# Queries on partitions for all heads of a decoder block, stores on GpSimd's queue, gating weights kept

## The chip, the cores and the metric

The kernel runs on one core of a Trainium2 chip. The metric is the device time of one execution in microseconds; the median of three runs is given. One further execution was profiled, and all rows of the trace come from it. TensorE multiplies matrices, VectorE, ScalarE and GpSimd work element by element, and SyncE only issues transfers; each engine takes its instructions in order and waits where a result is missing.

## What is computed

One decoder layer on 2048 tokens of width 1024 in float32. Half of the mixer is attention with eight heads of 64, each a mixture of three dilated windows; the other half is a spatial gating unit. A SwiGLU network follows. Each half is wrapped in RMS norms.

```python
DILATED_PATTERNS = ((128, 1), (512, 4), (2048, 16))
def dilated_mixture_attention(q, k, v):
    ...
    for window, dilation in DILATED_PATTERNS:
        o, lse = dilated_window_attention(q, k, v, window, dilation)
        ...
    wts = jax.nn.softmax(jnp.stack(lses, axis=0), axis=0)
    o = jnp.sum(wts[..., None] * jnp.stack(outs, axis=0), axis=0)
...
h = rms_norm(x, pre_mix_norm[l])
proj = h @ w_in[l]
q, k, v_a, u, v_s = jnp.split(proj, ...)
...
attn = dilated_mixture_attention(q, k, v_a)
sgu = spatial_gating(u, v_s, ...)
mixed = jnp.concatenate([rms_norm(attn, attn_out_norm[l]), rms_norm(sgu, sgu_out_norm[l])], axis=-1)
x = x + rms_norm(mixed @ w_out[l], post_mix_norm[l])
h = rms_norm(x, pre_ffn_norm[l])
f = (jax.nn.silu(h @ w_gate[l]) * (h @ w_up[l])) @ w_down[l]
x = x + rms_norm(f, post_ffn_norm[l])
```

## The kernel before

The tokens are cut into four blocks of 512 (m = 0 to 3), and the attention into two halves of 1024 queries (x = 0 for blocks 0 and 1, x = 1 for blocks 2 and 3). To keep float32 accuracy with a faster product, each operand is split into a high part and the rest (`w_hi`, `w_lo`; `ah`, `al`; `ph`, `pl`), and a dense product is three products: high by high, rest by high, high by rest. A weight block is loaded by `wtile` (L167) as `w_raw`, copied to `w_hi` by ScalarE and subtracted to `w_lo` by VectorE; where the same block is needed again, `w_lo` is stored in DRAM (`wc`) and comes back by `wcached` (L189). `group` (L204) runs the dense products of one projection (all of them have line L212) into four banks `d` and hands each bank to an `evac`.

The program has these parts. Up to 165 us of the span: in_proj of k, q and v for blocks 0 and 1. From 165 to 747 ("stage 2"): the gating unit of all blocks (`ip_su` L476, `ip_gate` L512), the reload of block 0's normalised input from `hD` (`ip_again` L397), in_proj of blocks 2 and 3, all merged with `tq_heads(0)`. From 747 to 1545 ("stage 3"): out_proj of blocks 0 and 1, the first three parts of the feed-forward network and the up projection of its second half, merged with `heads(1)`. Then out_proj of blocks 2 and 3, the last down projection, and from 1850 on a part that the change leaves alone (`st_up`, `st_down`).

The two halves of the attention are written in two ways. `heads(1)` (L1631) has keys on partitions: `scores` (L665) multiplies 256 queries at a time against a block of 128 keys (L728, L729), adds the mask (L736) and keeps a running maximum `macc`; `mix` (L753) subtracts the maximum, takes the exponential, splits into `ph` and `pl`, and multiplies with the values (L809, L811), again 256 queries at a time. `tq_heads(0)` (L1013) has queries on partitions: `tq_scores` (L934) multiplies 128 queries against up to 512 keys (L963, L964), VectorE reduces to a minimum per query and ScalarE takes the exponential with it; `tq_turn` (L974) transposes the weights by TensorE in blocks of 128 (L1003, L1006) and splits them, and `pv` (L1056, L1057) multiplies with the values, mostly 128 columns at a time. At the end of each pair of heads `tq_merge` (L1114) passes small tables through DRAM (`rr`, `tqC`, `ww`, then the weights `ws` and `wn`), which takes four transfers one behind the other.

A scheduler sets the order in which instructions stand on each engine. `merge` interleaves two generators by the numbers of steps given (L1652: 133 x 1.2 steps for the first heads, L1662), `high_priority` raises some instructions, and a tile's `bufs` says how many buffers it has: a load into a tile stands in the order where a buffer of it comes free. Every transfer, load or store, is issued by `dma` (L146, issue at L151) on SyncE. An evacuation of k, q or v writes into four `io` buffers and stores eight pieces per group of four banks (L447 to L464). `out_rows` (L1178) evacuates the rows of out_proj and of the down projection to `y`, adds the residual row `xr`, which it loads `ahead` rows in advance, and stores the result; in stage 3 there is one `xr` buffer and `ahead` is 1.

```python
            v.scalar_tensor_tensor(yj, yj, r, xs[i], ALU.mult, ALU.add)
            self.dma(dst[j * P:(j + 1) * P, 512 * n:512 * n + 512], yj)
            ...
            fetch(i + ahead)
```

Of the kernel before, what the change touches and what calls it, by code (L numbers as in the profile page):

```python
# [10 lines left out]
F32 = mybir.dt.float32  # L11
# [67 lines left out]
HP_Q = 200  # L79
# [5 lines left out]
XR = 1  # L85
T_LAG = 2
T_END = 3
HP_T = 0
# [4 lines left out]
R1 = 1.2  # L93
# [19 lines left out]
class Body:  # L113
# [38 lines left out]

    def rstd(self, ss, n, inv_n, eps, name, parts=P):
# [13 lines left out]
    def wtile(self, src, perm=False, shape=None, save=None, pool=None, bufs=None):  # L167
# [17 lines left out]
        if save is not None:  # L185
            self.dma(save, lo)
# [179 lines left out]
    def ip_load2(self, c, pool):  # L366

        self.seen[c] = True
        w_in = self.t["w_in"][0].rearrange("(k p) c -> k p c", p=P)
        kept = {}  # L370

        def load(k):
            kept[k] = self.wtile(w_in[k, :, c * 512:(c + 1) * 512], perm=c < 2, pool=pool, bufs=W_KEPT)
            return kept[k]

        def again(k):
            self.dma(self.wc[c][k], kept[k][1])
            return kept.pop(k)

        return load, again  # L380
# [9 lines left out]
    def ip_keep(self, m):  # L390

        for k in range(KT):
            for i in range(2):
                self.dma(self.hD[k, i], self.h[m][i][k])
                yield

    def ip_again(self, m):  # L397

        h = self.ip_tiles(m, self.ip)
        for k in range(KT):  # L400
            for i in range(2):
                self.dma(h[i][k], self.hD[k, i])
            yield
# [27 lines left out]
    def ip_kq(self, m, sec, load, tabs):  # L431
# [3 lines left out]
        def evac(b, ps):  # L435
# [14 lines left out]
            self.dma(scr[0][b * P:(b + 1) * P, :], oh)  # L450
            self.dma(scr[1][b * P:(b + 1) * P, :], ol)
# [3 lines left out]
    def ip_v(self, m, load):  # L455
        nc, pool, v = self.nc, self.ip, self.nc.vector

        def evac(b, ps):
            pv = ps.rearrange("p (h e d) -> p h e d", h=4, e=2)
            for e in range(2):  # L460
# [3 lines left out]
                self.dma(self.vD[m][e::2, b * P:(b + 1) * P, :].rearrange("h p d -> p h d"),  # L464
# [47 lines left out]
    def ip_gate(self, m):  # L512
# [4 lines left out]
        ws = pool.tile([P, 2, 8, P], F32R, name="ws", tag="big", bufs=4)  # L517
        self.dma(ws, self.wsD)
# [25 lines left out]
        for ft in range(4):  # L544
# [5 lines left out]
            self.dma(self.sT[m][ft], o)  # L550
# [11 lines left out]
    def attn_pools(self, pool):  # L562
        self.ap, self.lt = pool, "mt"
        self.cst = pool.tile([P, C_TRIL], F32, name="cst")
        self.dma(self.cst, self.t["consts"][:, 0:C_TRIL])

    def stacks(self, x, h):

        nc, pool = self.nc, self.ap
        nkm = 2 * (x + 1)  # L570

        def rows(scr):
            return scr.rearrange("(a h d) t -> h a d t", a=8, h=8)[h]

        qs = pool.tile([P, 4, 2, P], F32R, name="qs", tag="qs", bufs=1)
        ql = pool.tile([P, 4, 2, P], F32R, name="ql", tag="ql", bufs=1)
        ks = [pool.tile([P, TB], F32R, name="ks", tag="ks", bufs=4) for _ in range(nkm)]
        for mm in range(2):
            q = self.qT[2 * x + mm]
            for dst, src in ((qs[0:64], q[0]), (qs[64:128], q[0]), (ql[0:64], q[1]), (ql[64:128], q[1])):  # L580
                self.dma(dst[:, :, mm, :], rows(src))
        for m in range(nkm):
            for s in range(2):
                self.dma(ks[m][64 * s:64 * s + 64, :], rows(self.kT[m][s]))
        nf = 7 * x
        k1 = pool.tile([P, 8 + x, P], F32R, name="k1", tag="k1", bufs=1, padded_shape=[P, 9, P])
        for m in range(nf // 4, nkm):
            lo = max(nf, 4 * m)
            n = 4 * m + 4 - lo
            nc.gpsimd.tensor_copy(k1[:, lo - nf:lo - nf + n, :].rearrange("p j (r i) -> p j r i", r=4),  # L590
                                  ks[m].rearrange("p (r j i) -> p j r i", r=4, j=4)[:, 4 - n:4])
        return ks, k1, nf, qs, ql

    def values(self, x, h):

        pool = self.ap
        nkm = 2 * (x + 1)
        v4 = [pool.tile([P, 4, P], F32R, name="v4", tag="v4", bufs=4) for _ in range(nkm)]
        n0 = 0 if x == 0 else 7
        v1t = pool.tile([P, 8 * (x + 1) - n0, P], F32R, name="v1", tag="v1", bufs=1, padded_shape=[P, 9, P])  # L600
        v1 = {n: v1t[:, n - n0, :] for n in range(n0, 8 * (x + 1))}
        for m in range(nkm):
            self.dma(v4[m].rearrange("p r d -> p (r d)"), self.vD[m][h].rearrange("(i r) d -> i (r d)", r=4))
            lo = max(n0, 4 * m)
            cnt = 4 * m + 4 - lo
            if cnt > 0:
                src = self.vD[m][h].rearrange("(j i r) d -> r i j d", r=4, i=32)
                for r in range(4):
                    self.dma(v1t[32 * r:32 * r + 32, lo - n0:lo - n0 + cnt, :], src[r, :, 4 - cnt:4])
        return v4, v1  # L610

    def lanes(self, acc, op, name):
# [4 lines left out]
        tr = self.ap.tile([P, 1024], F32, name=name + "_t", tag=self.lt, bufs=1)  # L617
# [7 lines left out]
    def to_row(self, src, dst, name):  # L625
# [3 lines left out]
        self.dma(dst.rearrange("(b a) -> b a", a=32), t)  # L629

    @staticmethod
    def qview(u, a):

        if u[1][0] == "s":
            o = u[1][1] * 256 + u[1][2] * 128
            return a[:, o:o + u[2]]
        return a.rearrange("p (r c) -> p r c", r=4)[:, :, 32 * u[1][1]:32 * u[1][2]]

    @staticmethod
    def uview(u, a, off):  # L640
        s = a[:, off:off + u[2]]
        return s if u[1][0] == "s" else s.rearrange("p (r c) -> p r c", r=4)

    @staticmethod
    def twins(us):

        return len(us) == 2 and us[0][2] == us[1][2] == 256

    def fold(self, us, s, acc, op, seen):

        if us[0][1][0] == "s" and us[0][1][1] not in seen:
            seen.add(us[0][1][1])
            o = us[0][1][1] * 256
            if self.twins(us):
                self.nc.vector.tensor_tensor(acc[:, o:o + 256], s[:, 0:256], s[:, 256:512], op)
            else:
                self.nc.scalar.copy(acc[:, o:o + 128], s[:, 128:256])
                self.nc.vector.tensor_tensor(acc[:, o + 128:o + 256], s[:, 256:384], s[:, 0:128], op)
            return
        off = 0  # L660
        for u in us:
            self.nc.vector.tensor_tensor(self.qview(u, acc), self.qview(u, acc), self.uview(u, s, off), op)
            off += u[2]

    def scores(self, x, h, st):  # L665

        nc, v, pool = self.nc, self.nc.vector, self.ap
        ks, k1, nf, qs, ql = self.stacks(x, h)
        yield
        qf, qlf = (t.rearrange("p r m i -> p (r m i)") for t in (qs, ql))  # L670
        q3, ql3 = (t.rearrange("p r m i -> p r (m i)") for t in (qs, ql))
        n0 = 8 * x
        tiles = []

        def keys4(r, m):
            return ks[m][:, r * P:(r + 1) * P]

        def keys1(n):
            return k1[:, n - nf, :]

        for r in range(4):
            for pr in range(x + 1):
                us = []
                for m in (2 * pr, 2 * pr + 1) if pr < x else (2 * pr + 1, 2 * pr):
                    last = m == 2 * x + 1
# [1025 lines left out]
```

## Time and profile before

| | |
|---|---|
| median of three runs | 2573.8 us (2573.55 to 2574.82) |
| profiled execution | 2575.44 us |
| its span | 2573.7 us |
| TensorE busy | 2328.9 us, 90% |
| VectorE busy | 1639.1 us, 64% |
| ScalarE busy | 1185.9 us, 46% |
| GpSimd busy | 364.4 us, 14% |
| mean granted clock of TensorE | 0.958 |
| transfers, mean | 186 GB/s, all of the kernel's on one queue (q1) |

A share over the span is an average over stages with different limits, so it is read together with windows by stage. The tables of waits give, for an engine, which instruction it stood before and what ended the wait last. In a timeline an engine's instructions stand in the order of their starts; since products are pipelined, a product's own time is longer than its distance to the next start.

### The profile page before, as it was taken

The page shows a single profiled execution, that of the slowest core. Times are in us where ns is not written, and L with a number is a line of the kernel's source. Part 1 is how long each engine was busy: PE and PEld are TensorE (multiplying, and loading weights), DVE is VectorE, ACT ScalarE, POOL GpSimd, SP SyncE. Part 2 cuts the span into 40 slices and gives each one's busy share as a digit, 9 for nine tenths or more (in the row PEclk, how much of TensorE's full clock was granted, in tenths as well). Part 3 has the DMA queues.
Part 4 walks back from the last instruction along what each step waited for, and adds up shares of the span by engine and source line. Part 5 has one row for each costly group of instructions (what it writes and reads, how often), then busy time and mean ns, then how long its engine had stood idle before and what let it go on. Part 6 is the DMA issues. An engine that isn't in the chain of part 4 may idle for free. (4 is left out here: it accounts for less than half of the span.)

```text
span 2573.7 us, 33168 instructions
## 1 busy us (share of the span) xinstructions
PE 2328.9 (90%) x10685; PEld 1890.1 (73%) x10685; DVE 1639.1 (64%) x3209; ACT 1185.9 (46%) x2278; POOL 364.4 (14%) x338
## 2 busy tenths in 40 slices
PE   7997779989869799999999999998788899999996
PEld 6776667778757678887777887777677688887774
DVE  5524354534569996768899743657677767665566
ACT  6425677556525654535555533545322233334433
POOL 0000000000000000000000000001164567641011
PEclk9998889989989899999999999999999999999998
DMA  7867666776667565456655445776465533326554
GB/s 242 296 193 237 194 201 211 244 215 204 221 207 225 156 214 155 134 154 204 201 163 186 128 123 179 213 221 205 157 214 203 200 111 103 103 86 220 173 193 167
DMA packets 350910, 479.66 MB, mean 186 GB/s; under 512 B 33264, under 2 KB 177168, under 8 KB 350224
## 3 DMA queue, kind: packets, MB, share of 16 engines
q1 hardware_dynamic: 350736, 477.55, 59.1%
q8 instruction: 84, 1.38, 0.2%
q14 instruction: 90, 0.74, 0.1%
HBM read 367.74 MB, written 109.69 MB: 186 GB/s over the span
## 5 line engine op out<-in xcount | busy, mean ns | idle before, releaser
L183 ACT CAST w_hi<-w_raw 128x512 fp32r<-128x512 f32 x368 | 226.7, 618 | 319.7 <-PE d L212 235.0
L184 DVE TENSOR_TENSOR w_lo<-w_raw,w_hi 128x512 fp32r<-128x512 f32 x368 | 255.0, 696 | 183.5 <-ACT w_hi L183 177.3
L212 PE MATMUL d<-ah,w_hi 128*128 128x512 f32 x704 | 275.1, 392 | 1.6 <-ACT ah L338 1.6
L212 PE MATMUL d<-al,w_hi 128*128 128x512 f32 x704 | 275.8, 392 | 0.0
L212 PE MATMUL d<-ah,w_lo 128*128 128x512 f32 x704 | 275.4, 391 | 0.0
L1454 PE MATMUL d<-th,w_lo 128*128 128x512 f32 x616 | 247.3, 402 | 19.5 <-DVE w_lo L1345 19.5
L1454 PE MATMUL d<-th,w_hi 128*128 128x512 f32 x616 | 244.1, 396 | 14.1 <-ACT w_hi L1344 10.1
L1454 PE MATMUL d<-tl,w_hi 128*128 128x512 f32 x616 | 244.4, 397 | 0.0
L1345 DVE TENSOR_TENSOR w_lo<-raw,w_hi 128x512 fp32r<-128x512 f32 x187 | 148.6, 828 | 91.9 <-ACT w_hi L1344 90.9
L1344 ACT CAST w_hi<-raw 128x512 fp32r<-128x512 f32 x187 | 108.4, 618 | 158.3 <-PE d L1536 108.6
L212 PE MATMUL d<-w_hi,hh 128*128 128x512 f32 x384 | 157.2, 412 | 19.6 <-ACT w_hi L201 9.6
L212 PE MATMUL d<-w_lo,hh 128*128 128x512 f32 x384 | 157.1, 409 | 5.5 <-DMA w_lo<-wc 4.9
L212 PE MATMUL d<-w_hi,hl 128*128 128x512 f32 x384 | 154.9, 405 | 0.0
L1454 PEld LDWEIGHTS d<-th,w_lo 128*128 128x128 f32 x616 | 117.9, 191 | 50.3 <-DVE w_lo L1345 25.8
L212 PEld LDWEIGHTS d<-ah,w_hi 128*128 128x128 f32 x704 | 132.1, 188 | 27.1 <-ACT ah L338 1.8
L212 PEld LDWEIGHTS d<-ah,w_lo 128*128 128x128 f32 x704 | 132.3, 188 | 26.0
L212 PEld LDWEIGHTS d<-al,w_hi 128*128 128x128 f32 x704 | 132.3, 188 | 25.7
L212 PE MATMUL d<-w_hi,fl 128*128 128x512 f32 x352 | 139.9, 405 | 11.3 <-DVE fl L1312 11.2
L212 PE MATMUL d<-w_hi,fh 128*128 128x512 f32 x352 | 143.3, 407 | 5.5 <-ACT fh L1311 5.5
L1454 PEld LDWEIGHTS d<-th,w_hi 128*128 128x128 f32 x616 | 117.9, 191 | 40.6 <-ACT w_hi L1344 10.7
L212 PE MATMUL d<-w_lo,fh 128*128 128x512 f32 x352 | 140.6, 400 | 0.0
L1454 PEld LDWEIGHTS d<-tl,w_hi 128*128 128x128 f32 x616 | 118.0, 191 | 27.1
(312 smaller groups left out, 5473.5 us busy)
## 6 DMA issues: line engine op xcount, KB each, us to landing
w_raw<-in_w_in SPq DMA_DIRECT2D x136, 256.0 KB
w_lo<-wc SPq DMA_DIRECT2D x96, 256.0 KB
w_raw<-in_w_gate SPq DMA_DIRECT2D x88, 256.0 KB
w_raw<-in_w_up SPq DMA_DIRECT2D x88, 256.0 KB
w_raw<-in_w_down SPq DMA_DIRECT2D x88, 256.0 KB
araw<-fD SPq DMA_DIRECT2D x88, 256.0 KB
raw<-fS SPq DMA_DIRECT2D x77, 256.0 KB
w_raw<-in_w_out SPq DMA_DIRECT2D x64, 256.0 KB
```

The lines of the kernel that those rows point to most:

```text
L183: nc.scalar.copy(hv, rv)
L184: nc.vector.tensor_tensor(lv, rv, hv.bitcast(F32), ALU.subtract)
L212: nc.tensor.matmul(banks[b], lhsT, rhs, start=(k == 0 and j == 0), stop=(k == nk - 1 and j == len(ops) - 1))
L1344: nc.scalar.copy(hv, src)
L1345: nc.vector.tensor_tensor(lv, src, hv.bitcast(F32), ALU.subtract)
L1454: nc.tensor.matmul(ps, a[:, c], b, start=(k == 0 and n == 0), stop=(k == 3 and n == 2))
```

## The change

- `heads(1)` and all that belongs to it (`scores`, `mix`, `stacks`, `values`, `fold`) go; the second half of the attention runs as `tq_heads(1)` with 96 steps of scores (64 in `tq_heads(0)`).
- `tq_load` loads queries and keys; the copies `q1` of the queries and the loads of values move to the new `tq_near`. `qs` and `ql` have one buffer instead of two, and the loads for the next head stand later (behind the last step of the dilated part).
- A second way to issue a transfer, `put`, uses GpSimd's queue. It takes the stores of `w_lo`, of `hD`, of k, q, v, of the gating result, of the attention's result and its tables, of the rows and of the feed-forward network's middle, the reload of `hD`, and the whole chain of `tq_merge`: 406 issues. SyncE keeps 1669 of 2038.
- The gating weights (`wsD`, 1 MB) are loaded once into a tile of their own, instead of once for each block.
- The first heads get 133 x 1.25 steps instead of 133 x 1.2; the scores lose their raised priority (200 to 0) and the transposes get it (0 to 200).
- In stage 3 the residual rows are loaded three ahead and share five `tmp` buffers, instead of one `xr` buffer of their own and four `tmp`.

```diff
-R1 = 1.2
+R0 = 1.25
-HP_Q = 200
-HP_T = 0
+HP_T = 200
+HP_S = 0
+T_BUF = 5
...
+    def put(self, out, in_):
...
+        self.nc.gpsimd.dma_start(out, in_)
...
         if save is not None:
-            self.dma(save, lo)
+            self.put(save, lo)
...
-            self.dma(scr[0][b * P:(b + 1) * P, :], oh)
-            self.dma(scr[1][b * P:(b + 1) * P, :], ol)
+            self.put(scr[0][b * P:(b + 1) * P, :], oh)
+            self.put(scr[1][b * P:(b + 1) * P, :], ol)
...
-        ws = pool.tile([P, 2, 8, P], F32R, name="ws", tag="big", bufs=4)
-        self.dma(ws, self.wsD)
+        ws = self.ws
...
+        if x == 0:
+            self.ws = pool.tile([P, 2, 8, P], F32R, name="wgt")
+            self.dma(self.ws, self.wsD)
...
-            if b == 1 and h + 1 < NH:
+            if b == ns + 1 and h + 1 < NH:
                 loads[h + 1] = self.tq_load(x, h + 1)
...
-        self.dma(rr, T.rearrange("p s i -> p (s i)"))
+        self.put(rr, T.rearrange("p s i -> p (s i)"))
...
-        ahead = self.xr[2]
+        ahead = self.xr[3]
...
-        merge(w1, 4 * 50 + 24 + 4 * G, tq_heads(0), 133 * R1)
+        merge(w1, 4 * 50 + 24 + 4 * G, tq_heads(0), 133 * R0)
...
-        b.ff_pools(ff, fa, ff, (ff, "xr", 1))
+        b.ff_pools(ff, fa, ff, (ff, "tmp", T_BUF, 3))
...
-                    _merge(b.ffn_down(0), 49, b.ffn_prep(1), 12), b.ffn_up(1)), 269, heads(1), (8 * 29 + 1) * R2)
+                    _merge(b.ffn_down(0), 49, b.ffn_prep(1), 12), b.ffn_up(1)), 269, tq_heads(1), 197 * R2)
```

The first place is SyncE's queue in stage 2 where block 0's input (`hh`, `hl`) has come back and the gating begins; `w_raw` is a weight block, `v` the values of a head, `ws` the gating weights. Before:

```order
L151 DMA hl<-hD 128x512
L151 DMA hh<-hD 128x512
L151 DMA hl<-hD 128x512
L151 DMA w_raw<-in_w_in 128x512
L151 DMA w_lo<-wc_0_130 128x512
...
L151 DMA v_2488<-vD_94 32x4x128 x4
L151 DMA v_2487<-vD_95 128x512
L151 DMA v_2488<-vD_95 32x4x128 x4
L151 DMA ws<-wsD 128x2048
L151 DMA w_raw<-in_w_in 128x512
```

After, the reload of `hh` and `hl` and the gating weights are gone from this place, and weight blocks stand ahead of the values:

```order
L151 DMA v_2393<-vD_95 128x512
L151 DMA v_2394<-vD_95 32x4x128 x4
L151 DMA lng<-in_sgu_ln_gain 128x512
L151 DMA lnb<-in_sgu_ln_bias 128x512
L151 DMA w_raw<-in_w_in 128x512
L151 DMA w_lo<-wc_0_130 128x512
L151 DMA w_raw<-in_w_in 128x512
L151 DMA w_lo<-wc_1_131 128x512
L151 DMA w_raw<-in_w_in 128x512 x2
L151 DMA w_lo<-wc_2_132 128x512
```

What moved: the reload stands on GpSimd's queue now, and the one load of the gating weights stands in the first part.

The second place is SyncE's queue at the change from stage 2 to stage 3: `vD` are the last stores of block 3's values, `rA` the norm of the first heads, `qs`, `ql` and `ks` the first queries and keys of the second heads, `araw` the input of out_proj. Before:

```order
L151 DMA rA_333<-an_w 32x32
L151 DMA ql<-qT_1_91 64x4x128 x2
L151 DMA qs<-qT_0_92 64x4x128 x2
L151 DMA vD_97<-io 128x4x128 x4
L151 DMA ql<-qT_1_93 64x4x128
L151 DMA vD_97<-io 128x4x128 x4
L151 DMA ql<-qT_1_93 64x4x128
L151 DMA ks<-kT_0_78 64x1x512
L151 DMA ks<-kT_1_79 64x1x512
L151 DMA araw<-sT_324 128x512 x4
L151 DMA grow<-in_post_mix_norm 128x512
```

And after:

```order
L151 DMA w_lo<-wc_7_121 128x512
L151 DMA w_raw<-in_w_out 128x512
L151 DMA qs<-qT_0_90 64x4x128 x2
L151 DMA ql<-qT_1_91 64x4x128 x2
L151 DMA qs<-qT_0_92 64x4x128 x2
L151 DMA ql<-qT_1_93 64x4x128 x2
L151 DMA ks<-kT_0_78 64x1x512
L151 DMA ks<-kT_1_79 64x1x512
L151 DMA ks<-kT_0_80 64x1x512
L151 DMA ks<-kT_1_81 64x1x512
L151 DMA ks<-kT_0_82 64x1x512
```

What moved: the stores `rA` and `vD` are no longer among the loads; they stand on GpSimd's queue.

The third place is TensorE's queue inside the first up projection, where dense products (`d`) and the second heads alternate. Before, a score or value product has 256 columns:

```order
L212 MATMUL d_9486<-ah_8457,w_lo_9634 128x512
L809 MATMUL pv_9402<-ph_9526,v4_9342 128x256
L212 MATMUL d_9487<-ah_8456,w_hi_9639 128x512
L811 MATMUL pv_9402<-pl_9527,v4_9342 128x256
L809 MATMUL pv_9402<-ph_9526,v4_9343 128x256
L811 MATMUL pv_9402<-pl_9527,v4_9343 128x256
L212 MATMUL d_9487<-al_8464,w_hi_9639 128x512
L212 MATMUL d_9487<-ah_8456,w_lo_9640 128x512
```

After (L220 is the dense product, L726 and L729 are transposes, L780 and L781 value products):

```order
L220 MATMUL d_9754<-al_8460,w_hi_9759 128x512
L729 MATMUL qk_9794<-ident_345,S_9700 128x4x32
L726 MATMUL qk_9794<-ident_345,S_9700 128x128
L220 MATMUL d_9754<-ah_8452,w_lo_9760 128x512
L220 MATMUL d_9754<-ah_8453,w_hi_9759 128x512
L220 MATMUL d_9754<-al_8461,w_hi_9759 128x512
L220 MATMUL d_9754<-ah_8453,w_lo_9760 128x512
L220 MATMUL d_9755<-ah_8452,w_hi_9759 128x512
L220 MATMUL d_9755<-al_8460,w_hi_9759 128x512
L780 MATMUL pv_9728<-ph_9651,v1_8794 128x4x32
L220 MATMUL d_9755<-ah_8452,w_lo_9760 128x512
L781 MATMUL pv_9728<-pl_9652,v1_8794 128x4x32
```

What moved: between the same dense products there now stand transposes and products of 128 columns (4 x 32).

## Rows read from the trace of the kernel before

**Rows 1.** Windows by stage: length, busy us of each engine, granted clock, DMA share, GB/s.

```profile
165.00:747.00 582.00, 485.31 (x2416) 394.93 (x2415) 267.71 (x734) 331.07 (x735) 21.30 (x34) 0.92 0.70 214
747.00:1545.00 798.00, 755.48 (x3639) 624.25 (x3640) 642.55 (x1372) 396.22 (x685) 24.20 (x86) 0.98 0.56 171
```

**Rows 2.** TensorE's waits in 165 to 747: releaser, us in total, times, longest.

```profile
PE qk L728 <- DMA ks<-kT: 14.0, 2, 12.9
PE d L212 <- ACT w_hi L201: 9.6, 1, 9.6
PE qk L527 <- DMA ws<-wsD: 9.1, 1, 9.1
PE qk L1003 <- ACT S L971: 6.0, 1, 6.0
PE d L212 <- DVE io L449: 5.9, 4, 1.7
PE d L212 <- DMA w_lo<-wc: 4.9, 1, 4.9
PE d L212 <- ACT w_hi L198: 1.7, 1, 1.7
PE qk L1006 <- DVE tqM L969: 1.0, 1, 1.0
```

**Rows 3.** TensorE's waits in 747 to 1545.

```profile
PE d L212 <- DVE y L1212: 14.6, 2, 14.3
PE qk L728 <- DVE S L736: 9.1, 13, 1.3
PE qk L728 <- DMA ks<-kT: 7.8, 2, 6.5
```

**Rows 4.** SyncE's timeline, two places: start, us, the transfer issued, count.

```profile
245.85 0.62 SPq L151 DMA_DIRECT2D w_raw<-in_w_in  x1
262.27 0.35 SPq L151 DMA_DIRECT2D ws<-wsD  x1
...
721.52 2.63 SPq L151 DMA_DIRECT2D vD<-io  x4
724.85 1.39 SPq L151 DMA_DIRECT2D ks<-kT  x2
```

**Rows 5.** Windows of two stretches: a stop of TensorE, and behind another.

```profile
717.60:731.00 13.40, 0.49 (x3) 0.09 (x1) 1.70 (x4) 1.49 (x4) 0.00 (x0) 0.65 0.90 251
851.90:856.00 4.10, 4.10 (x12) 3.30 (x13) 3.81 (x17) 1.29 (x4) 0.00 (x0) 0.65 0.47 125
```

**Rows 6.** TensorE's timeline: start, us, line, operation, shapes.

```profile
405.38 0.27 PE L1003 MATMUL qk<-ident,S 128*128 128x128 f32 x1
405.41 0.48 PE L212 MATMUL d<-w_hi,hh 128*128 128x512 f32 x1
405.72 0.39 PE L212 MATMUL d<-w_lo,hh 128*128 128x512 f32 x1
405.95 0.40 PE L212 MATMUL d<-w_hi,hl 128*128 128x512 f32 x1
...
408.24 0.28 PE L1056 MATMUL pv<-ph,v 128*128 128x256 f32 x1
408.36 0.28 PE L1057 MATMUL pv<-pl,v 128*128 128x256 f32 x1
408.48 0.22 PE L1056 MATMUL pv<-ph,v 128*128 128x128 f32 x1
408.54 0.28 PE L1057 MATMUL pv<-pl,v 128*128 128x128 f32 x1
408.65 0.44 PE L212 MATMUL d<-w_hi,hh 128*128 128x512 f32 x1
408.93 0.40 PE L212 MATMUL d<-w_lo,hh 128*128 128x512 f32 x1
```

**Rows 7.** GpSimd's groups by line: count, busy us and mean ns, idle before.

```profile
L1475 POOL TENSOR_TENSOR fs<-fs 128x512 f32<-128x512 f32 x11 | 19.1, 1740 | 0.0
```

More of the change, by code (lines that the diff above doesn't have):

```diff
@@ L151, in dma @@
         self.nc.sync.dma_start(out, in_)
+    def put(self, out, in_):
+        if out.dtype == F32R:
+            out = out.bitcast(F32)
+        if in_.dtype == F32R:
+            in_ = in_.bitcast(F32)
+        self.nc.gpsimd.dma_start(out, in_)
     def rstd(self, ss, n, inv_n, eps, name, parts=P):
@@ L376, in again @@
         def again(k):
-            self.dma(self.wc[c][k], kept[k][1])
+            self.put(self.wc[c][k], kept[k][1])
             return kept.pop(k)
@@ L559, in i4 @@
         return ap.rearrange("p (i r) -> p i r", r=4)
[L562 to L610, printed above, removed]
     def lanes(self, acc, op, name):
@@ L645, in twins @@
[L645 to L663, printed above, removed]
@@ L874, in attn_norm @@
+        self.put(dst.rearrange("(b a) -> b a", a=32), t)
     def attn_norm(self, x):
@@ L903, in tq_load, with tq_near @@
                 self.dma(ks[64 * s:64 * s + 64, m, :], rows(self.kT[m][s]))
-        q1 = []
-        for src in (qs, ql):
+        return [qs, ql, None, ks, None, None]
+    def tq_near(self, x, h, ld):
+        nc, pool = self.nc, self.ap
+        nkm = 2 * (x + 1)
+        ld[2] = []
+        for src in ld[:2]:
             d = pool.tile([P, 8, P], F32R, name="q1", tag="q1", bufs=2)
@@ L909, in tq_load @@
                                       src[:, :, mm, :].rearrange("p r (j i) -> p j r i", j=4))
-            q1.append(d)
-        v4 = [pool.tile([P, 4, P], F32R, name="v4", tag="v4", bufs=2 * nkm) for _ in range(nkm)]
+            ld[2].append(d)
+        v4 = [pool.tile([P, 4, P], F32R, name="v4", tag="v4", bufs=4) for _ in range(nkm)]
         n0 = 0 if x == 0 else 7
-        v1t = pool.tile([P, 8 * (x + 1) - n0, P], F32R, name="v1", tag="v1", bufs=2)
+        v1t = pool.tile([P, 8 * (x + 1) - n0, P], F32R, name="v1", tag="v1", bufs=2 - x)
         for m in range(nkm):
@@ L921, in tq_load @@
                     self.dma(v1t[32 * r:32 * r + 32, lo - n0:lo - n0 + cnt, :], src[r, :, 4 - cnt:4])
-        return qs, ql, q1, ks, v4, {n: v1t[:, n - n0, :] for n in range(n0, 8 * (x + 1))}
+        ld[4:] = v4, {n: v1t[:, n - n0, :] for n in range(n0, 8 * (x + 1))}
     def tq_banks(self, x):
@@ L942, in tq_scores @@
         todo = []
-        with self.tc.high_priority(HP_Q):
+        with self.tc.high_priority(HP_S):
             for u in units:
@@ L1238, in out_proj @@
             for kt in order:
-                raw = pool.tile([P, TB], F32, name="araw", tag="tmp", bufs=4)
+                raw = pool.tile([P, TB], F32, name="araw", tag="tmp", bufs=T_BUF)
                 if kt < 4:
@@ L1319, in load_d @@
         def load_d(k, n):
-            s = pool.tile([P, TB], F32, name="araw", tag="tmp", bufs=4)
+            s = pool.tile([P, TB], F32, name="araw", tag="tmp", bufs=T_BUF)
             self.dma(s, self.fD[m][k])
@@ L1629, in tq_heads @@
             yield from b.attn_norm(x)
-        def heads(x):
-            st, pair = {}, {}
-            yield from b.scores(x, 0, st)
-            for h in range(NH):
-                ahead = b.scores(x, h + 1, st) if h + 1 < NH else iter(())
-                for step in b.mix(x, h, st, pair):
-                    yield
-                    if step:
-                        next(ahead, None)
-                        yield
-                for _ in ahead:
-                    yield
-            yield from b.attn_norm(x)
-        atx = attn(0, b.tq_pools)
+        atx = attn(0, lambda pool: b.tq_pools(0, pool))
         G = 8 + 2 * GATE_LAG
```

256 lines of the change are left out of this document (23 added, 233 removed).

## Prediction

> **What bounds the kernel now.** I read the windows by stage first, because the busy share over the whole span mixes stages that have different limits. Two stages are touched. From 165 to 747 us (stage 2) TensorE is busy for 485 of 582 us at a granted clock of 0.92; from 747 to 1545 us (stage 3) for 755 of 798 us at 0.98 [rows 1]. No other engine comes near in either: VectorE has 268 and 643 us, ScalarE 331 and 396. So stage 3 is TensorE's own work with 43 us of idle time, and stage 2 has 97 us of idle time and a low clock on top. Whoever adds work to TensorE in stage 3 pays for it nearly in full; whoever removes VectorE's work there gains only what TensorE waits for it.
>
> Next I read what ended TensorE's waits. In stage 2, seven entries end at a load or at a weight split that waits for its load, from the 14.0 of `ks<-kT` to the 1.7 of `w_hi` L198, 45.5 us together [rows 2]. A further eight belong to the attention steps of heads(0), from the 6.0 of `S` L971 to the 1.0 of `tqM` L969, 18.5 us. In stage 3 one wait of 14.3 for `y` L1212 stands out, then 9.1 for the mask addition `S` L736 of the old heads and 7.8 for `ks<-kT` [rows 3].
>
> Last I looked for why the loads are late, in SyncE's timeline. Every transfer is issued there, in order. The weight block behind the 9.6 for `w_hi` L201 is issued only at 245.85 and the gating weights behind the 9.1 only at 262.27; at the change of stages, four `vD` stores leave at 721.52 and the key loads behind them at 724.85 [rows 4], while TensorE has stood since 717.6 [rows 5]. A store that waits for its result holds back every load behind it.
>
> **The change, part by part.** The sum is made against the profiled execution, 2575.4 us, which is 1.6 above the median.
>
> (a) *Stores on GpSimd's queue, gating weights kept.* SyncE keeps the loads; stores, the reload of `hD` and tq_merge's chain of small transfers go to GpSimd, 406 issues in all. Three of four loads of the gating weights go. What can be had is the 45.5 us and stage 3's 7.8, together 53, and the clock. If the 485 busy microseconds of stage 2 ran at stage 3's 0.98 instead of 0.92, they would be 30 shorter; the load stops are just under half of the idle time, so I count 15. The bound is 68. I take four fifths, **-54**: at the change of stages the 16 DMA engines were 0.90 busy while TensorE stood [rows 5], so part of that wait is the transfers themselves.
>
> (b) *Rows by threes.* In out_rows each residual row was loaded into the only `xr` buffer after the row before had been finished, so rows came one by one and the next projection's `y` waited: 14.6 us [rows 3], and the 4.1 us behind it ran at 0.65 [rows 5], another 1.4. Three loads ahead hide behind the row before. **-15**; the `tmp` buffers that they now share (five) could take some of it back.
>
> (c) *Old heads gone.* The wait for `S` L736, 9.1, goes with its line: **-9**. VectorE's other work of the old heads ran beside TensorE and gives nothing.
>
> (d) *TensorE's work in stage 3.* From the two orders: 720 products of 256 columns and 96 of 128 go. In their place come for the scores 64 of 512 columns, 64 of 384, 96 of 256 and 64 of 128; for the values 64 of 256 and 576 of 128; and 352 transposes. Costs are distances from start to start [rows 6]. A product of 512 columns takes 0.23 (405.72 to 405.95), one of 256 takes 0.12 (408.24 to 408.36 to 408.48; 0.118 in the mean of that piece), and a pair of 128 columns pushes what follows: from 408.48 the next starts are 408.54, 408.65 and 408.93, 0.45 less the 0.23 of the dense product between, so 0.11 each. A transpose at 405.38 sees 405.41 and then 405.72, 0.34 less 0.23, again 0.11. For 384 columns I estimate 0.175 from its neighbours. Removed: 720 x 0.118 + 96 x 0.112 = 96. Added: scores 14.7 + 11.2 + 11.3 + 7.2 = 44, values 7.6 + 64.5 = 72, transposes 352 x 0.11 = 39; 155. Net **+59**, and since stage 3 has little idle time, all on the path. The lower bound reads the pair as 0.06 each (408.48 to 408.54) and a transpose as 0.07: 544 x 0.052 + 352 x 0.04 = 42 less, so +17. I take 0.11, because in both places the delay arrives at the dense product behind.
>
> (e) *Waits of the new heads.* Each step is a chain (product, minimum, exponential, transpose, split, product). Stage 2 has 64 such steps and 18.5 us of waits; stage 3 gets 96, so 28 at most. The 6.0 is one stop beside the gating; without it 12.5 x 1.5 = 19. More dense products lie between two steps here, and transposes now go ahead of scores, so I take about half, **+10**, with ends 0 and 28.
>
> (f) *Price of a store on GpSimd.* No GpSimd transfer is in the trace. The nearest rows are SyncE's own issue, 0.35 to 0.70 each [rows 4], and GpSimd's arithmetic, up to 1.74 [rows 7]. I take SyncE's, so nothing: GpSimd is busy for some 20 us per stage [rows 1]. What is queued behind a waiting store is other stores, the copies of near queries and tq_merge's chain; who waits for them is an evacuation of k, q or v, whose 4 `io` buffers come back after 8 stores. TensorE waits 5.9 for it now, over four times [rows 2]. At 1.74 instead of 0.5 the eight stores take 10 us more, at most half of it late for the next group: 12 groups x 5 = +60 as the upper end. Below nothing is excluded, since SyncE's issue is not what that wait ends with.
>
> (g) *Shift of steps (1.25 for 1.2), buffers of `qs`, `v1`:* these move the same work; taken at nothing. The one `qs` buffer is refilled while a head's near part still runs, since only the copies `q1` are read there.
>
> Sum: -54 - 15 - 9 + 59 + 10 = -9, so 2566 profiled, **2565** against the median.
>
> **The rivals.** *The loads stay late and the steps wait* (slower). If DMA time and not the queue ends half of the waits in (a), and the new heads bring their full 28, the sum is -34 - 15 - 9 + 59 + 28 = +29: **2603**. For it speaks the DMA share of 0.90 in the stop at 717.6 [rows 5]; against it that the key loads were issued 7 us after that stop had begun [rows 4, 5]. With the rest as forecast, it decides at two thirds of the 68: below that the kernel is slower.
>
> *Stores are dear on GpSimd* (slower). Half of the +60 in (f) gives -9 + 30 = +21: **2595**. It decides at about 0.9 us per store, where half of the bound eats the gain.
>
> *Where a transfer is issued does not matter* (slower). If moving the stores frees nothing, (a) keeps the gating weights' 9.1 and some 3 of clock: -12 - 15 - 9 + 59 + 10 = +33: **2607**. This is also the case in which the change does not do what it says. The Trainium skill, page DMA: Bandwidth & Descriptors, section Issuing engines are not separate DMA queues, says that transfers from several engines end up on the same DMA engines and that a second issuer saves only the sequencer's time, which is usually small. By that rule the time would be 2607; the trace here speaks for more, since SyncE spends its time waiting for results ahead of loads, not in issuing [rows 4].
>
> *Everything comes back* (faster). All 68, 16 for the rows, no waits of the new heads: -68 - 16 - 9 + 59 = -34: **2540**; with narrow products half way to their lower bound, 2520. For it speaks that all four late loads stand behind waiting stores.
>
> **How the numbers follow.** The forecast with some 12 us around it has 0.36; everything back 0.22, loads late 0.20, dear stores 0.09, no matter 0.08, and 0.05 for things worse or better than these. A run of this kernel can tell about 0.2%, 5 us. From the forecast 0.24 is faster and 0.12 same; with everything back faster comes to 0.47; the slower cases and a little of the sums near nothing leave 0.15 same and 0.38 slower. The range goes from 2525, between everything back and its cheaper products, to 2608, which takes in the three slower cases. Both signs hold much, and the forecast's own range is 2553 to 2578.
>
> **What would show it.** (a) holds if the waits for `w_hi` L201, for `ws` and for `ks<-kT` (9.6, 9.1, 14.0) are gone, and stage 2 up to the first out_proj is 50 or more shorter at a clock of 0.95 or above; it fails if new waits for `ks<-kT` or `w_raw` of 5 us or more stand there. (b) holds if no wait for `y` over 3 us is left before 1500. (d) holds if the busy time of the part with heads(1) grows by 50 to 65 us; 20 would mean that narrow products overlap. (e) is the sum of waits on ScalarE and VectorE lines of the new heads in that part. (f) shows in how long GpSimd's issues last and in the waits for `io` L449. The prediction is wrong if stage 2 shrinks by less than 30, or stage 3 grows by other than 20 to 60.

## The result, and the profile after

The changed kernel takes 2669.6 us in the median (2667.8 to 2681.3, four runs) against 2574.3 us: a ratio of 1.038, 95% interval 1.035 to 1.041, so 95 us slower. The forecast was 2565 and the range ended at 2608. The profiled execution is 2667.8 us with a span of 2665.9.

To see where the time went I use a division that does not depend on where a stage begins. The dense products (`d` at L212, L220 after) are 5856 in both kernels and stand in almost the same order, so the start of the n-th of them, counted from 0, can be compared. Products number 560 (near the end of in_proj of v for block 1), 1920 (the first of out_proj) and 4680 (shortly behind the last second head) bound three parts, worked out from the timelines of TensorE:

| part, us | before | after | difference |
|---|---|---|---|
| up to product 560 | 167.6 | 186.4 | +18.8 |
| 560 to 1920 (stage 2) | 564.6 | 576.4 | +11.9 |
| 1920 to 4680 (stage 3) | 806.9 | 869.7 | +62.8 |
| behind it | 1034.6 | 1033.4 | -1.2 |

Each column, here and below, comes from the one profiled execution of a kernel. Thirteen kernels of this document leave the queue up to product 560 as it was, and need 166.9 to 170.8 us for it; the part behind product 4680 goes from 1029.8 to 1037.9 over all kernels. A difference of some 4 us in one part therefore says nothing by itself.

The windows of these three parts, before (columns as in [rows 1]):

```profile
0.00:167.59 167.59, 148.24 (x658) 117.82 (x659) 74.97 (x158) 81.52 (x157) 0.70 (x6) 0.99 0.75 251
167.59:732.15 564.56, 475.01 (x2380) 387.09 (x2378) 258.63 (x721) 326.26 (x729) 20.39 (x32) 0.92 0.71 216
732.15:1539.07 806.92, 757.26 (x3639) 625.08 (x3639) 645.91 (x1374) 399.12 (x690) 25.11 (x88) 0.97 0.57 171
```

and after:

```profile
0.00:186.37 186.37, 153.27 (x658) 120.94 (x658) 75.40 (x158) 81.49 (x157) 47.94 (x90) 0.95 0.66 226
186.37:762.82 576.45, 481.81 (x2394) 394.66 (x2392) 261.20 (x727) 334.16 (x739) 117.01 (x201) 0.90 0.69 207
762.82:1632.50 869.68, 825.87 (x4089) 690.93 (x4089) 444.99 (x936) 449.71 (x876) 86.99 (x155) 0.97 0.54 164
```

In stage 3 TensorE's busy time is 69 us up; its idle time is 44 us now against 50. In the first two parts busy time hardly changes at the same products (+5 and +7, at a clock of 0.95 and 0.90 instead of 0.99 and 0.92), and idle time grows instead of shrinking: 33 against 19, and 95 against 90. GpSimd, once nearly idle there, is busy for 48 and 117 us, mostly with issues.

What ends TensorE's waits after the change, in 165 to 754 us and, behind the dots, in 754 to 1632 (compare [rows 2, 3]):

```profile
PE d L220 <- DVE io L457: 13.6, 5, 6.5
PE qk L534 <- DVE pl L733: 10.0, 1, 10.0
PE qk L726 <- ACT S L694: 8.1, 4, 4.7
PE pv L780 <- DVE a L793: 7.3, 2, 5.9
PE d L220 <- DVE io L471: 7.1, 3, 5.9
PE d L220 <- ACT w_hi L191: 5.6, 1, 5.6
PE d L220 <- DMA w_lo<-wc: 1.1, 2, 0.7
...
PE qk L686 <- DMA ks<-kT: 9.1, 2, 8.9
PE qk L686 <- DVE tqM L692: 8.8, 6, 3.0
```

The waits that the prediction wanted gone are gone or smaller: `ws` has vanished, `w_lo<-wc` fell from 4.9 to 1.1, the 9.6 for `w_hi` L201 (L209 now) is not in the list, and of the 14.0 and 7.8 for `ks<-kT` 9.1 are left. But others have taken their place: the evacuations' `io` (13.6 and 7.1 for 5.9), the attention's own chain (`pl`, `S`, `a`, `tqM`), and a weight block at another line (`w_hi` L191, L183 before). The gating product that had waited 9.1 for `ws` (L527, now L534) waits 10.0 for `pl`. By the prediction's own signs (a) fails: stage 2 is 12 us longer instead of 50 shorter, and single waits of 8.9 for `ks<-kT` and 5.6 behind a weight load stand there.

### The profile page after: what moved, and what is told of

The parts are those of the page before. It is cut to its first block, busy times and chain, and to the rows that moved or that the text cites. A ratio compares the mean times of both kernels' runs of the same rounds, so it can differ in the third digit from the quotient of the medians.

```text
span 2665.9 us, 34169 instructions
## 1 busy us (share of the span) xinstructions
PE 2411.6 (90%) x11149; PEld 1967.0 (74%) x11149; DVE 1435.4 (54%) x2757; ACT 1243.5 (47%) x2474; POOL 586.7 (22%) x688
## 5 line engine op out<-in xcount | busy, mean ns | idle before, releaser
L191 ACT CAST w_hi<-w_raw 128x512 fp32r<-128x512 f32 x368 | 226.5, 618 | 355.5 <-PE d L220 257.8
L220 PE MATMUL d<-ah,w_hi 128*128 128x512 f32 x704 | 279.5, 397 | 3.6 <-DVE sil L1025 2.1
L220 PE MATMUL d<-al,w_hi 128*128 128x512 f32 x704 | 279.7, 397 | 0.0
L220 PE MATMUL d<-ah,w_lo 128*128 128x512 f32 x704 | 279.3, 397 | 0.0
L220 PE MATMUL d<-w_hi,hh 128*128 128x512 f32 x384 | 158.1, 414 | 26.0 <-DVE io L457 11.6
L694 ACT ACTIVATE S<-S,tqM 128x256 f32<-128x256 f32 (+3 forms) x256 | 135.0, 528 | 93.2 <-DVE tqM L692 92.2
L220 PE MATMUL d<-w_lo,hh 128*128 128x512 f32 x384 | 157.6, 410 | 3.4 <-DVE w_lo L192 2.3
L220 PE MATMUL d<-w_hi,hl 128*128 128x512 f32 x384 | 157.4, 412 | 0.0
L220 PEld LDWEIGHTS d<-ah,w_hi 128*128 128x128 f32 x704 | 133.6, 190 | 29.4 <-DVE sil L1025 2.7
L220 PEld LDWEIGHTS d<-ah,w_lo 128*128 128x128 f32 x704 | 134.1, 190 | 27.4 <-DVE w_lo L192 0.4
L692 DVE CUSTOM_DVE_ANT_0 S<-qk,cstq 128x256 f32<-128x256 f32 (+3 forms) x256 | 108.7, 448 | 83.5 <-PE qk L687 82.2
L220 PEld LDWEIGHTS d<-al,w_hi 128*128 128x128 f32 x704 | 134.1, 191 | 25.9
L220 PE MATMUL d<-w_hi,fl 128*128 128x512 f32 x352 | 141.1, 403 | 10.7 <-DVE fl L1036 10.6
L220 PE MATMUL d<-w_hi,fh 128*128 128x512 f32 x352 | 143.2, 407 | 4.0 <-ACT fh L1035 4.0
```

What stands on the lines that cost most here:

```text
L191: nc.scalar.copy(hv, rv)
L220: nc.tensor.matmul(banks[b], lhsT, rhs, start=(k == 0 and j == 0), stop=(k == nk - 1 and j == len(ops) - 1))
L692: v.tensor_tensor_reduce(out=so, in0=ps[:, off:off + w], in1=mask, scale=-0.125, scalar=BIG, op0=ALU.add, op1=ALU.min, accum_out=M[:, c:c ...
L694: nc.scalar.activation(so, so, AF.Exp, scale=-1.0, bias=M[:, c:c + 1], accum_out=D[:, c:c + 1])
```

## The experiments

Each kernel below was timed against the kernel before on the same chip; the ratio is to that, with its 95% interval. Parts are those of the table above.

**Which part of the change costs?** e1 is the kernel before with `self.put` wherever the change has it; e2 has the new second heads and, with them, the split of a head's loads (`tq_load`, `tq_near`); e3 only the rows; e4 is the changed kernel with

```diff
-        self.nc.gpsimd.dma_start(out, in_)
+        self.nc.sync.dma_start(out, in_)
```

> The kernel before with one part of the change alone: the stores, the reload of hD and tq_merge's chain are issued on GpSimd, nothing else is changed. Theory A (two separate causes: GpSimd's queue costs some 30 us up to 750, the new second heads some 60 behind it): 20 to 40 us slower than before, 2595 to 2615, with the loss up to 750 and the first of it before 110. Theory B (the queue is the whole cause, also in stage 3): 60 to 95 us slower. Theory C (the second heads are the whole cause): no difference, or faster by up to 30.

> The kernel before with the second heads rewritten (queries on partitions) and the loads of a head split as in the changed kernel; every transfer stays on SyncE, the gating weights are loaded four times, one xr buffer, the old priorities and 133 x 1.2 steps. Theory A: 50 to 70 us slower than before, 2625 to 2645, nearly all behind 730. Theory B: within 15 us of before. Theory C: about 95 us slower, 2670.

> The kernel before with the residual rows of stage 3 loaded three ahead into five shared buffers, nothing else. If the price of 15 us for the wait for y was right: 10 to 16 us faster than before, 2558 to 2564. If the wait moves on to the shared buffers: no difference.

> The changed kernel with every transfer issued on SyncE again; the heads, the gating weights, the priorities, the steps and the rows stay changed. Theory A: 30 to 45 us faster than the changed kernel, 2625 to 2640. Theory B: 2575 to 2590. Theory C: 2665 to 2680, no faster than the changed kernel.

Measured: e1 1.016 (1.012 to 1.020), 2616.5 us; e2 1.014 (1.009 to 1.019), 2612.2; e3 0.997 (0.995 to 0.998), 2568.4; e4 1.010 (1.007 to 1.014), 2600.9.

| part, us | before | e1 queue | e2 heads | e3 rows | e4 all on SyncE | after |
|---|---|---|---|---|---|---|
| up to 560 | 167.6 | 186.9 | 168.0 | 168.1 | 167.9 | 186.4 |
| 560 to 1920 | 564.6 | 579.9 | 553.5 | 564.0 | 546.2 | 576.4 |
| 1920 to 4680 | 806.9 | 812.6 | 853.3 | 805.7 | 850.9 | 869.7 |

B and C fall: the queue alone costs, and so do the heads alone. Of theory A (two separate causes) that much holds, but not its sizes: e2 is 33 us slower than before where it had 50 to 70, e4 69 faster than the changed kernel where it had 30 to 45, and the two causes are not independent. In the changed kernel the queue costs 18.5 + 30.3 + 18.8 = 68 us (after less e4), in the old one 40 (19.3 + 15.3 + 5.7). With the new second heads there are eight chains of tq_merge instead of four, and half of them stand in stage 3, which fits the 13 more there (e5 below); why the queue costs 15 more in stage 2 no run separates. In e2 the first two parts became 11 us shorter, which nobody had expected; e15 below tells why.

**Why does the queue cost up to product 560?** In the first 46 us GpSimd has nothing else to do, so stores to `hD` and `wc` leave as soon as their data is there, from 18.7 on. Before, they stood on SyncE behind the loads of block 1; those to `hD` left from 28.6 to 83.6. The window 20 to 35 before:

```profile
20.00:35.00 15.00, 15.00 (x78) 12.13 (x77) 11.02 (x25) 14.81 (x34) 0.00 (x0) 1.00 0.81 283
```

and after 20 to 38 and 38 to 46, with ScalarE's wait for weights from 20 to 46 and TensorE's for `xs`:

```profile
20.00:38.00 18.00, 18.00 (x89) 14.42 (x87) 10.88 (x24) 12.19 (x28) 8.39 (x16) 1.00 1.00 387
38.00:46.00 8.00, 0.66 (x3) 0.18 (x1) 3.43 (x15) 6.37 (x15) 4.53 (x9) 0.74 1.02 398
...
ACT w_hi L191 <- DMA w_raw<-in_w_in: 6.3, 5, 2.9
...
PE qk L344 <- ACT xs L339: 7.6, 2, 7.3
```

The share of the transfer engines (second last column) is 1.00 where it was 0.81. ScalarE waits 6.3 us for loads of weights where none is listed before, TensorE stops 7.3 us, and the clock is at 0.74 in the stop. e6 puts these two groups of stores back on SyncE in the changed kernel; e9 moves only the 16 `hD` stores in the kernel before; e10 issues those on ScalarE's queue (`self.nc.scalar.dma_start`).

> The changed kernel with two groups of stores back on SyncE: w_lo to wc, and hh and hl to hD; the rest stays on GpSimd. Theory E (these stores leave at once on an empty queue and share the transfer engines with the loads of the next block): the 18 us lost up to 110 us are back, 15 to 25 us faster, 2645 to 2655. If instead each GpSimd transfer delays VectorE or ScalarE by itself: 5 us at most come back before 110, since the kT stores stay.

> The kernel before with one thing changed: the 16 stores of hh and hl to hD are issued on GpSimd. Theory E (they leave at once and share the transfer engines with the loads of block 1): a stop of TensorE for xs of 4 us or more near 38, 5 to 15 us slower than before. If the w_lo stores are what collides: no stop, within 4 us of before.

> As e9, with these 16 stores issued on ScalarE's queue, which is a hardware queue like SyncE's. Theory E (what counts is that they no longer stand behind loads, not who issues them): the same stop for xs and a loss within 5 us of e9's. Rival (transfers written by GpSimd are dearer): no stop, within 4 us of before.

e6: 1.030 (1.027 to 1.033), 2656.8 us, so 13 to 20 back. The share in 20 to 38 is 0.74, the stop for `xs` is gone, and at product 240 only 10.4 of the 18.4 us are lost; but by product 560 it is 18.8 again, through waits for `io` (one of 5.1 us at 111). e9 has the share and the stop:

```profile
20.00:38.00 18.00, 18.00 (x91) 14.52 (x90) 10.65 (x23) 11.27 (x24) 8.18 (x16) 1.00 1.00 384
...
PE qk L344 <- ACT xs L339: 6.8, 1, 6.8
```

It is 10.6 us behind at product 240 and 10.8 at 560; over the whole kernel 1.0015 (0.9995 to 1.0035), so much of it is made up later. The collision is shown where it happens, since share and stop come and go with these stores; the cause of the whole 18 us it is not. Up to product 560 of e6 GpSimd issues only the stores of k, q and v, and against e4, where nothing is moved, these alone lose as much as all groups together (186.4 against 167.9). TensorE's waits for `io` up to there are 3.5 us in e4, and in e6:

```profile
PE d L220 <- DVE io L457: 12.0, 6, 5.1
```

So there are two losses, stores that meet loads and `io` buffers that come back later, and they do not add. e10 has a stop of 2.3 us for `xs` and one of 3.9 for `hl` behind it; it is 8.6 us behind at product 240, 5.6 at 560, and 1.002 (1.001 to 1.004) in all. It does not test what it was made for: ScalarE has issued five of the 16 stores by 38 us, where GpSimd has issued all in e9, and the share in 20 to 38 is 0.81.

One rival no run takes out: with the queue, the order of the instructions changes too. Of ScalarE's 157 instructions up to product 560 all stand in the old order in e4, but 137 in e9, 126 in e10 and 124 in e1 (longest common sequence of the timelines). What is measured is a moved store together with the order that comes with it.

**tq_merge's chain.** Its transfers depend on each other, and each hop now passes GpSimd's queue. e5 puts the chain (and the small store of the norm) back on SyncE; e11 does that and what e6 does.

> The changed kernel with tq_merge's chain of small transfers (rr, tqC, ww, ws, wn) and the norm's row back on SyncE; all stores stay on GpSimd. Theory D (the chain is late on GpSimd, VectorE stands in front of un<-un,wn and holds the new heads): 25 to 40 us faster than the changed kernel, 2630 to 2645, and VectorE's waits for wn, ws and tqC, 86 us there, fall below 30. Theory E (the stores' bytes in early transfers are the whole cost of the queue): within 8 us of the changed kernel.

> The changed kernel with both groups back on SyncE: tq_merge's chain (e5) and the stores to wc and hD (e6). If the two add: 60 to 70 us faster than the changed kernel, 2605 to 2615, which is what e4 had left within 15. If the remaining stores (k, q, v, rows, middle of the network) cost much too: above 2620.

VectorE's waits for the tables after the change, over the whole span:

```profile
DVE un L883 <- DMA wn<-ww: 43.7, 7, 12.7
DVE tqm L859 <- DMA tqC<-rr: 31.4, 7, 9.7
DVE a L882 <- DMA ws<-ww: 10.7, 7, 6.1
```

and in e5:

```profile
DVE un L883 <- DMA wn<-ww: 14.8, 2, 11.3
DVE tqm L859 <- DMA tqC<-rr: 13.4, 4, 9.5
```

e5: 1.021 (1.019 to 1.024), 2632.9 us, 37 faster than the changed kernel (43 by the ratios), and 86 us of waits have become 30, 1.6 for `ws` included. Stage 2 is 560.9 us, 15 shorter, and stage 3 848.9, as in e4: in stage 3 the chain is the whole cost of the queue. Part of it is that the hops are longer on GpSimd: from the end of `tqT` to the start of `tqm` the eight chains take 11.5 us in the mean, 9.8 in e5, and from the last write of `tqW` to `un` 13.1 in the median, 11.4 in e5 (13.7 in the mean of either, since two chains of e5 take 22). With some 1.7 us in each half that is 27 of the 56 us, an estimate. The rest fits where `un` stands: in e5 it stands behind other work of VectorE and finds its tables there in six of eight cases, in the changed kernel it waits in seven. How the 37 us divide between hop and order is open. e11: 1.015 (1.013 to 1.017), 2619.4: 50 faster than the changed kernel (58 by the ratios), about the sum of e5 and e6 (37 and 13, or 43 and 20), though not the 60 expected. The 12 (by the ratios) to 18 us to e4 remain with the other stores.

**The price of the new heads.** e7 is e2 without the second heads' transposes:

```diff
-        nc.scalar.copy(ph[:, :w], tp[:, :w])
+        nc.scalar.copy(ph[:, :w], tp[:, :w] if x == 0 else s[:, :w])
```

> The kernel of e2 (second heads rewritten, all on SyncE) with the transposes of the second heads left out: the weights go to the value products untransposed, so the attention of the second half of the tokens is not computed. It measures term (d). If a transpose costs 0.11 us on the path, 440 + 128 less 216 = 352 of them give 39 us, and a little more for the shorter chain: 39 to 48 faster than e2, 2565 to 2573. If they are hidden beside other work: within 10 us of e2.

Stage 3 of e2 and of e7:

```profile
721.48:1574.73 853.25, 818.39 (x4104) 679.80 (x4105) 449.02 (x942) 432.23 (x866) 17.90 (x28) 0.98 0.56 168
```

```profile
720.90:1528.45 807.55, 778.63 (x3752) 652.38 (x3753) 448.76 (x942) 428.37 (x862) 21.69 (x28) 0.97 0.60 177
```

e7: 0.992 (0.989 to 0.995), 2559.3 us, 53 faster than e2 (39 to 48 were expected). TensorE's busy time in stage 3 falls by 39.8 us for 352 transposes, 0.113 each, and the part by 45.7. From before to e2 busy time grew by 818.4 - 757.3 = 61, where the working had 59.

**The rows.** In e3 the stop of 14.3 us for `y` is gone, but stage 3 is only 1.2 us shorter. These waits, none of which was among those of 1.6 us or more before, stand there instead:

```profile
PE qk L336 <- DVE po_y L159: 4.2, 1, 4.2
PE pv L809 <- DVE at L851: 4.0, 1, 4.0
PE pv L809 <- DVE a L846: 3.8, 1, 3.8
PE d L212 <- ACT ah L1250: 3.1, 1, 3.1
```

They sum to 15.1. Of what e3 gains in all (9 us by the ratio) 4.8 lie behind product 4680, where such a difference says nothing, so its place is not shown.

**Why did the load waits not pay?** e8 is the kernel before with all that had not cost in e4: split loads, gating weights kept, rows by threes, steps and priorities; e12 the same with the old steps and priorities; e15 only the split. e13 is e12 with the stores of block 3's values on GpSimd, so that none stands among the first loads of the second heads.

> The kernel before with the parts that cost nothing by the runs so far: the split of a head's loads, gating weights kept, rows by threes, 133 x 1.25 steps, transposes ahead of scores; old second heads, every transfer on SyncE. By the lags of e4 up to 720 (18 us gained) and the 10 of e3: 20 to 30 us faster than before, 2545 to 2560. Rival (the gain up to 720 came from the new second heads' first loads): 10 to 15 faster, 2560 to 2570.

> The kernel of e8 with the old steps (133 x 1.2) and the old priorities of scores and transposes. If its gain comes from the loads (split, gating weights kept) and the rows: within 6 us of e8. If it comes from the steps and priorities: 10 or more slower than e8, 2562 or above.

> The kernel before with only the split of a head's loads (keys and queries of the next head behind the dilated part, one buffer of qs). With the gating weights kept and the rows by threes it makes e12, 33 us faster than before on the same chip; rows alone gave 9. If the split carries the larger part of the rest: 12 to 20 us faster than before. If the gating weights carry it: within 6 us of before.

> The kernel of e12 with only the eight stores of block 3's values on GpSimd, so that no vD store stands among the first loads of the second heads; there are no early loads for them to meet. Theory F (a waiting store is what makes those loads late, as the prediction said): the wait for ks<-kT at the change of stages, 16 us with its second part in e12, falls by 6 or more, and the kernel is 5 to 12 us faster than e12. Theory G (the loads then stand behind weight loads that wait for a buffer, and behind their own transfer): the wait stays within 4 us, the time within 5 us of e12.

e8: 0.989 (0.987 to 0.992), 2551.5 us. e12: **0.984 (0.981 to 0.987), 2541.7 us**, faster than both kernels and 10 faster than e8, which neither expectation had. e15: 0.995 (0.993 to 0.998), 2564.5. Stage 2 takes 549.3 in e15 and 533.1 in e12: the split gives 15, the gating weights 16 more (the rows gave nothing there), and the steps and priorities cost 6 (539.5 in e8) and 7 more in stage 3 (807.9 against 800.9).

The split shows what had held the gating weights back. SyncE's queue ahead of them before, and, behind the dots, in e15, where every store is still on SyncE:

```profile
235.95 2.13 SPq L151 DMA_DIRECT2D wc<-w_lo  x3
254.37 7.78 SPq L151 DMA_DIRECT2D v<-vD  x10
262.27 0.35 SPq L151 DMA_DIRECT2D ws<-wsD  x1
...
243.17 0.43 SPq L151 DMA_DIRECT2D ws<-wsD  x1
```

Between the `wc` stores and 262.7 SyncE issues no store at all, only the reload, weights, and a head's queries, keys and values. With these loads spread, `ws` leaves 19 us sooner and no wait for it is left in e15.

e13: 0.986 (0.983 to 0.989), 2539.9. The wait for the keys in e12 and in e13:

```profile
PE qk L727 <- DMA ks<-kT: 17.3, 3, 12.0
```

```profile
PE qk L735 <- DMA ks<-kT: 12.7, 3, 7.8
```

It falls by 4.6 us, between what theories F and G had, and the time doesn't change: the waits for `io` grow by 3.3 (10.4 to 13.7), stage 2 is 9.5 us longer and stage 3 5.6 shorter. The changed kernel shows why a load gains little from the stores' leaving. SyncE's waits for a dense product, before (165 to 732) and after (186 to 763), with three issues at the change of stages:

```profile
SPq L151 <- PE d L212: 86.3, 59, 5.4
```

```profile
SPq L151 <- PE d L220: 222.8, 76, 47.4
...
718.66 2.73 SPq L151 DMA_DIRECT2D w_raw<-in_w_in  x2
730.87 1.02 SPq L151 DMA_DIRECT2D w_lo<-wc  x2
743.06 5.08 SPq L151 DMA_DIRECT2D ks<-kT  x8
```

With the stores gone SyncE runs on to the next weight load that has no buffer and stands there, 223 us instead of 86: from 721.4 to 730.9 it waits for the buffer of `w_lo`, and the queries and keys behind it leave at 735 and 743, just before TensorE needs them at 745.0; it stops for the keys until 754.2. By these waits the buffers set the pace of that queue, and the stores only took part of the same time.

**Which stores lose in stage 2?** e14 is e12 with GpSimd's queue for what comes later, without the chain and `w_lo`; e16, e17 and e18 move one group of it each.

> The kernel of e12 with GpSimd's queue for the stores of k, q and v of blocks 2 and 3, of the gating and attention results, of the rows and of the network's middle, and for the reload of hD; what is stored up to 165 us, w_lo and tq_merge's chain stay on SyncE. If the queue gains once early collisions and the chain are out: 10 to 25 us faster than e12, 2517 to 2532. If it gains nothing or loses: 2538 or above.

> The kernel of e12 with only the reload of hh and hl from hD on GpSimd. If this is where e14 loses (its lag opens behind the reload): 10 to 25 us slower than e12, 2552 to 2567. If not: within 6 us of e12.

> The kernel of e12 with only the stores of k, q and v of blocks 2 and 3 on GpSimd. If the io buffers come back later from GpSimd: 8 to 20 us slower than e12, with the wait for io L449's line above its 10.4 us. If these stores are free there: within 6 us of e12.

> The kernel of e12 with only the stores of the gating result and of the attention's result on GpSimd; they stand on SyncE for results of ScalarE and VectorE (20 and 11 us there). If a waiting store holds loads back: 5 to 15 us faster than e12. If not: within 5 us of e12.

e14: 0.996 (0.995 to 0.998), 2568.9 us; e16: 0.994 (0.992 to 0.995), 2558.6; e17: 0.988 (0.986 to 0.990), 2544.4; e18: 0.987 (0.986 to 0.988), 2541.4. Stage 2 takes 533.1 in e12, and 564.8, 548.6, 540.7 and 537.6 in these: +31.7 for all, +15.5, +7.6 and +4.5 for the groups, which sum to 27.6. No group gains. e17 and e18 are at the edge of what can be told: 3 and 0 us slower than e12 by the medians, 11 and 9 by the ratios, which were taken on another chip. Stage 2 of e12 and of e14:

```profile
168.92:701.97 533.05, 465.75 (x2379) 381.69 (x2378) 258.58 (x721) 328.02 (x730) 20.93 (x32) 0.95 0.74 223
```

```profile
167.67:732.45 564.78, 483.20 (x2398) 394.62 (x2396) 260.76 (x727) 335.94 (x737) 72.77 (x125) 0.91 0.70 212
```

Idle time goes from 67 to 82 us and the clock from 0.95 to 0.91. The reload is the largest. On SyncE it stands behind three weight loads, here in e12:

```profile
220.30 1.29 SPq L151 DMA_DIRECT2D w_raw<-in_w_in  x3
221.68 0.38 SPq L151 DMA_DIRECT2D hh<-hD  x1
```

In e16 it starts 8 us sooner on GpSimd and ten of its 16 issues are out when TensorE stops for 6.1 us for a weight block (window of stage 2, the wait, and the first of the reload's issues):

```profile
169.13:717.77 548.64, 471.53 (x2379) 385.50 (x2378) 258.26 (x721) 331.55 (x733) 30.10 (x48) 0.93 0.72 217
...
PE d L220 <- ACT w_hi L191: 6.4, 2, 6.1
...
213.93 0.71 POOL L159 DMA_DIRECT2D hh<-hD  x1 [3.39 <-PE d L220]
```

That is the order of the first part again: what is needed later goes first. That it is the whole of the 15.5 us is argued, not shown. In e17 the waits for `io` have grown by as much as stage 2, from 10.4 us in e12 (165 to 731):

```profile
PE d L220 <- DVE io L457: 17.8, 7, 4.8
```

For the few us of e18 no cause was tried.

## Why the prediction was wrong

- **(a), the step that failed.** It wanted -54 from the loads. Moving the stores was taken as a gain of some 40, and it is a loss of 68 in the changed kernel (e4 to after). The argument went from "the load is issued behind a store that waits" [rows 4] to "without the store it is issued in time", for all four late loads. Of the loads shown in [rows 4] the first half is true of the keys at 724.85 alone: ahead of the weight block SyncE had issued only loads for 8 us, the reload above all, and ahead of the gating weights for 24 us (238.1 to 245.85 and 262.27). The second half fails for the keys: in the changed kernel the next neighbour in the queue, a weight load without a buffer, waits instead (721.4 to 730.9).
- **The gating weights** are -12 in the rival and -16 measured (e15 to e12), but not by the rival's way: the wait of 9.1 for `ws` that it counted is already gone in e15. That the sizes agree is luck.
- **The rival that came nearest** was that it doesn't matter who issues (2607): e4, where nothing is moved, is at 2601. The Trainium skill's rule behind it (DMA: Bandwidth & Descriptors, Issuing engines are not separate DMA queues) is that transfers of all issuers run on the same 16 DMA engines and interleave. The share of 1.00 at 20 to 38 us, with stores from GpSimd beside loads from SyncE, agrees. That an earlier store delays the loads in front of TensorE, the rival lacked.
- **(f), the price of a store, taken at nothing.** The issue was right (0.54 us for `kT`, 0.75 for `vD` in the timeline, 0.5 taken). But `io` does come back later, the way that the text priced at up to +60 and then left out: up to 765 us TensorE waits 29.0 us for it in the changed kernel, 8.4 in e4. And two things have no price in it: tq_merge's chain behind the stores, which it names (37 us by e5), and the loads that the old order had protected from the stores, which it does not (e9).
- **(b)** -15 was wrong in place and size: -1 in stage 3, -9 in all (e3). Other waits of 15 us stood behind the one removed.
- **(c), (d), (e).** (d) held: 59 forecast, 61 in busy time; transposes 0.11 forecast, 0.113 measured. The waits came out cheaper: in e2 stage 3 is 46 us longer, so its idle time fell by 15 (806.9 less 757.3 is 50, 853.3 less 818.4 is 35) where -9 + 10 = +1 stood. That stage 3 without the queue came out at +44 (e4) for the 45 written is thus luck: two errors of 14 and 16 cancel, here and in (b).
- **(g)** taken at nothing: the split of a head's loads gives 15 us in stage 2 (e15), steps and priorities cost 6 there (e8 to e12).

What stays open: how the 18 us up to product 560 divide between the meeting of stores and loads, the `io` buffers and the changed order; how the chain's 37 us divide between its hops and the place of `un` in VectorE's order; why the queue costs 15 us more in stage 2 of the changed kernel than of the old one; and the few us of e18.

## What to carry to other kernels

A queue on which loads and stores stand in one order also paces them; before a store is taken out of it, ask which load it will then overtake, and what the next instruction in the queue waits for, since a load behind a store is only early without it if nothing else holds it. Read in the queue's timeline what really stands ahead of a late load: in stage 2 it was mostly other loads here, and spreading these gained 15 us where moving the stores gained nothing. A chain of dependent small transfers is not helped by a queue with fewer issues in it: on GpSimd (406 issues) it cost 37 us more than on SyncE (1783 in e5), and the engine that waits for its end stands in order for everybody. A change of many parts is best split by the time between the same instructions in both traces: here it gave each part's price to some 4 us.

## What the runs showed of the hardware

Transfers from GpSimd, with KB each and the median from issue to landing in us:

```profile
rr<-tqT POOLq DMA_DIRECT2D x8, 32.0 KB, 4.1
tqC<-rr POOLq DMA_DIRECT2D x32, 4.0 KB, 4.1
ww<-tqW POOLq DMA_DIRECT2D x32, 4.0 KB, 3.0
wn<-ww POOLq DMA_DIRECT2D x16, 256.0 KB, 4.8
fD<-sil POOLq DMA_DIRECT2D x44, 256.0 KB, 2.8
hl<-hD POOLq DMA_DIRECT2D x8, 256.0 KB, 8.0
```

In the median, the transfers of 4 KB in the chain land 3.0 and 4.1 us after their issue, and groups of 256 KB anywhere from 2.8 to 8.0. Four hops of the chain come to 16 us by these medians (4.1 + 4.1 + 3.0 + 4.8, an estimate), beside VectorE's work between them. The Trainium skill (DMA: Bandwidth & Descriptors, Anatomy of one DMA — SWDGE (gpsimd) path) gives a fixed cost of about 2 us per transfer on this path; the 3.0 and 4.1 here, beside other transfers, are above it. A transpose of 128 x 128 float32 costs TensorE 0.113 us between dense products (e2 less e7), half as much as a product of 512 columns (0.23 in [rows 6]).
